# Cosine-similarity attention on one core: five score banks with exponentials of three and two tiles, joint row sums, and a scale scratch inside a value bank

## The chip, the cores and the metric

The kernel runs on one core of a Trainium2 chip. The metric is the device time of one execution in microseconds. A core has TensorE (PE, with its weight loads listed as PEld), VectorE (DVE), ScalarE (ACT), GpSimd (POOL) and SyncE (SP), which here only issues transfers. Each engine works through its own list of instructions in order, and the lists are tied together by semaphores. PSUM is used in eight banks of 512 float32 columns by 128 partitions.

## The reference

Q, K and V are (8, 12, 512, 64) in float32, tau is 0.1.

```python
Q_norm = Q / (np.linalg.norm(Q, axis=-1, keepdims=True) + 1e-10)
K_norm = K / (np.linalg.norm(K, axis=-1, keepdims=True) + 1e-10)
scores = np.einsum('bhqd,bhkd->bhqk', Q_norm, K_norm) / tau
weights = np.exp(scores - np.max(scores, axis=-1, keepdims=True))
weights = weights / (np.sum(weights, axis=-1, keepdims=True) + 1e-10)
return np.einsum('bhqk,bhkd->bhqd', weights, V).astype(np.float32)
```

The scores are at most 10 in size, so the kernel takes the exponential without subtracting the maximum.

## The kernel before

The 96 heads are worked in 48 pairs s of two heads h. The 512 rows of a head lie as four tiles of 128. For a pair the steps are these, with the names under which the program keeps them:

- LD, LV: Q, K and V of the pair come in by DMA on SP's queue (256 KB each). VC casts V to bf16 on POOL and sets it beside a column of ones.
- SQ: the squares of Q and K, mostly one POOL instruction over 1024 columns (line 395).
- SSQ and RED: the sums of squares over 64 columns. For K, PE adds eight strided slices with an identity matrix as weights into columns 320 to 383 of one of the two value banks (SSQ, line 416), and DVE reduces the remaining 8 to 1 (RED, line 423). For Q, DVE reduces the squares directly (line 427). Only the K sums of pairs 43 and 47 are taken directly too.
- NEW: the reciprocal square root of the sums of a group of pairs (sizes 1, 1, 1, 1, then 2, later 4), in eight or so small DVE instructions of a Newton iteration (lines 450 to 465). The iterate lives in a PSUM bank of its own, `n_bank`, where PE never writes. Groups 0 and 1 use a logarithm and an exponential on ACT instead (NRMS, LOG, lines 283 to 285 and 439 to 448).
- SCL: Q times its scale on DVE (line 482), K times its scale on POOL for 38 pairs and on DVE for nine (`K_ON_DVE`).
- TR and EVA: PE transposes both (line 488), DVE copies them out of PSUM (line 496, `qt`).
- SCO: scores of one key tile c for both heads, two matmuls with 64 rows each (line 590), into two of the four banks of `sc_ps`; the two sets of two banks take turns.
- EXP: ACT reads both banks and writes 1024 columns of `et` (line 606). The last tile of the last pair is cut in three pieces (line 601); the tiles of pair 0 are taken one head at a time, with K's scale as a column (line 582). One tile, (43, 3), is not done on ACT but as a polynomial on DVE and POOL.
- PV: values, four key tiles for each of four query tiles, 128x65 (line 626), into value bank h (`o_ps`); column 64 holds the sum of weights. RCP takes its reciprocal (line 638), NRM scales into `ob` (line 643), ST writes 256 KB back.

A score group waits for the exponential that used its banks last, and for EVA. A group of values waits for the exponentials of its pair and, for its first tile, for the NRM (and RED, where a sum was put there) that used the bank before:

```python
bank_free[s, h] = before[b]
before[b] = [("NRM", s, h)] + ([("RED",) + attached[s, h]] if (s, h) in attached else [])
```

The order on every engine is written out by hand as a list of numbers (`ORDER`); nothing is reordered at run time. PE opens with nine warming matmuls of 512 columns (line 209). In the head, ACT squares parts of pairs 0 and 1 and does the norms of pair 0 before the exponentials run.

Of the kernel before, what the change touches and what calls it, by code (L numbers as in the profile page):

```python
# [108 lines left out]
def bass_cosine_similarity_attention_kernel(  # L109
# [26 lines left out]
    et = [sb(f"et{i}", [128, NT, 2, SEQ], bf16) for i in range(R_ET)]  # L136
# [15 lines left out]
    sc_ps = nc.alloc_psum_tensor("scps", [128, 4, SEQ], f32)  # L152
# [5 lines left out]
    n_bank = nc.alloc_psum_tensor("nps", [128, 512], f32)  # L158
    n_ps = n_bank[:, 0 : R_X * MOST].rearrange("p (r x) -> p r x", r=R_X)
# [62 lines left out]
    slots = sorted((START + PERIOD * (s + 1) + 0.9 * PV_AT[4 * h + 3] + 0.05 + late(s), s, h) for s in range(NP - 1) for h in range(2))  # L222
    chunks = [(s, c) for s in range(NP) for c in range(NT) if (s, c) not in OFF]
    off_of = {s: c for s, c in OFF}
    poly_groups = {group[s] for s in off_of}
    turn_user, free_user = {}, []
    for (s, c), turns in OFF.items():
        for h in range(2):
            if turns[h] >= 0:
                turn_user.setdefault(turns[h], []).append((s, h))  # L230
            else:
                free_user.append((s, h))
    session, attached, early = {}, {}, []
    for s, w in sorted(((s, w) for s in range(NP) for w in range(2) if on_pe(s, w)), key=lambda j: (due_red(j[0]), j)):
        at = due_red(s) + 0.3
        if s < EARLY:
            early.append((s, w))
            continue
        due, i, h = next(x for x in slots if x[0] >= at and (x[1], x[2]) not in attached)
        attached[i, h] = (s, w)  # L240
        session[s, w] = (h, due, [("PV", i, h, NT - 1)])
    before = [[("EVA", 0, 1, 0), ("EVA", 0, 1, 1)], []]
    for s, w in sorted(early):
        b = w if s >= ONE_BANK else 0
# [4 lines left out]
    before["n"] = [("SCL", NP - 1, 0)] + [("X",) + u + (1,) for u in free_user]  # L249
    place = lambda s, h: VALUE_BANK.get((s, h), h if s < NP - 1 else (0, 1, "t")[h])  # L250
    for s in range(NP):
        for h in range(2 if s < NP - 1 else 3):
            b = place(s, h)
            bank_free[s, h] = before[b]
            before[b] = [("NRM", s, h)] + ([("RED",) + attached[s, h]] if (s, h) in attached else [])
    values = {0: o_ps[0], 1: o_ps[1], "t": x_ps, "n": n_bank[:, :]}

    def head0(TF):
        for h in range(2):
# [5 lines left out]
            if CAST0[h] == "act":  # L265
# [3 lines left out]
            P.add(("CST", 0, h), CAST0[h], "cst" + CAST0[h], at, [("LD", 0, 1, h)], emit)  # L269
            r_ps = sc_ps[:, 1, 0:4] if h == 0 else n_ps[:, 0, 0:4]  # L270
# [53 lines left out]
    def root(s, w):  # L324
# [3 lines left out]
        return 7 if w == 0 or s in K_ON_DVE else 6  # L328
# [11 lines left out]
    def together(s, dst, g):  # L340
        bank, due, before = session[s, 1]

        def ssq(e):
            for k in range(8):
                last = e.matmul(
                    out=o_ps[bank][:, 320:448], lhsT=ident[:, :], rhs=sq[s % R_SQ][:, :, 8 * k : 8 * k + 8],
# [6 lines left out]
                  out=dst, in_=o_ps[bank][:, 320:448].rearrange("p (w g e) -> p w g e", w=2, e=8), axis=AX.X, op=ALU.add))  # L353

    def pair(s):
# [73 lines left out]
        xg, tg, yg = xs[g % R_X][:, 0 : 2 * m], ts[g % R_X][:, 0 : 2 * m], n_ps[:, g % R_X, 0 : 2 * m]  # L429
# [19 lines left out]
        elif s == first[g]:  # L449
# [6 lines left out]
            def up(dst, lo, hi, c):  # L456
# [8 lines left out]
                7: up(yg, 0, 2 * m, c_g) if on_dve else up(rq_g, 0, m, c_g)}  # L465
            done = None
            for k in news(g):
                needs = [done] if k else reds + [("SCL", i, w) for i in past for w in range(2) if w == 0 or i in K_ON_DVE]
                if k == 0 and g == R_X:
# [41 lines left out]
    def exps(s, c):  # L511
        if s < 0:
            return []
        if s == NP - 1 and c == NT - 1:
            return [("EXP", s, c, k) for k in range(3)]
        if s == 0:
            return [("EXP", s, c, h) for h in range(2)]
        return [("Y", s, last_step(s, c)) if (s, c) in OFF else ("EXP", s, c)]

    def poly(s, c, at):  # L520
# [6 lines left out]
        for h in range(2):  # L527
            users = turn_user[turns[h]] if turns[h] >= 0 else free_user
            bank = x_ps if turns[h] >= 0 else n_bank[:, :]
            after = ("EVA", turns[h]) if turns[h] >= 0 else ("SCL", NP - 1, 0)  # L530
# [35 lines left out]
    def rest(s):  # L566
# [3 lines left out]
        for c in range(NT):  # L570
# [3 lines left out]
            if s == 0:  # L574
                for h in range(2):
                    rows = slice(64 * h, 64 * h + 64)
                    P.add(("SCO", 0, c, h), "pe", "sco1", 0.5 * (c + NT * h),
                          [("EVA", 0, w, h) for w in range(2)] + ([("EXP", 0, c, 0)] if h else []) + ([("SCL", 0, 0, 0)] if c == 1 else []),
                          lambda e, c=c, rows=rows: e.matmul(
                              out=sc_ps[:, c, :], lhsT=qt[iqt][rows, 1, c, :], rhs=qt[iqt][rows, 0, :, :], start=True, stop=True))  # L580
                    P.add(("EXP", 0, c, h), "act", "exps", 0.5 * (c + NT * h), [("SCO", 0, c, h), ("NRMS", 0, 1, h), "table"],
# [3 lines left out]
            turn = chunks.index((s, c))  # L585
            b = turn % 2

            def sco(e, c=c, b=b):
                for h in range(2):
                    last = e.matmul(  # L590
                        out=sc_ps[:, 2 * b + h, :], lhsT=qt[iqt][64 * h : 64 * h + 64, 1, c, :],
                        rhs=qt[iqt][64 * h : 64 * h + 64, 0, :, :], start=True, stop=True)
                return last

            used = [("EXP", 0, 2 * c + i, 1) for i in range(2)] if turn < NT + 2 else exps(*chunks[turn - 2])
            P.add(("SCO", s, c), "pe", "sco", T0 + 0.9 * c, [("EVA", s)] + used, sco)
            if last_pair and c == NT - 1:
                for k, (h, lo, hi) in enumerate(PIECES):
                    P.add(("EXP", s, c, k), "act", "exp1" if hi - lo == NT else "exph", T0 + 0.9 * c + 0.3 * k,
                          [("SCO", s, c)] + [key("PV", s - R_ET, i, NT - 1) for i in range(2)],  # L600
                          lambda e, c=c, b=b, h=h, q=slice(128 * lo, 128 * hi): e.activation(
                              out=et[iet][:, c, h, q], in_=sc_ps[:, 2 * b + h, q], func=ACT.Exp, scale=math.log(2.0) / UNIT if group[s] in poly_groups else inv_tau))
                continue
            P.add(("EXP", s, c), "act", "exp", T0 + 0.9 * c,
                  [("SCO", s, c)] + [key("PV", s - R_ET, h, NT - 1) for h in range(2)] + ["table"],
                  lambda e, c=c, b=b: e.activation(  # L606
# [261 lines left out]
```

## Time and profile before

| | |
|---|---|
| median of 3 runs | 190.34 us (189.74 to 190.72) |
| profiled execution | 189.61 us, its span 187.9 us |
| granted clock of PE | 0.998 |
| busy: PE / DVE / ACT / POOL | 175.1 / 169.3 / 181.8 / 160.9 us |
| exponentials of 1024 columns | 186 |
| value products / score products / sums on PE | 1504 / 374 / 384 in the trace |
| read and written | 37.75 MB and 12.58 MB |

In the rows of the profile a group stands as: line, engine, operation, output<-input, shapes, xcount, then busy time of the group in us, mean duration of one in ns, and idle time of the engine just before them with what ended it. In a row of the timeline: start and length in us from the start of the span, engine, line, tiles, and how many instructions were merged. Durations of neighbours overlap on ACT, PE and DVE, so a pitch is read from starts or from busy time over count. In a row of stretches: the stretch, its length, the busy time of PE, PEld, DVE, ACT and POOL with instruction counts, the granted clock, the busy share of DMA and GB/s.

### The profile page before, as it was taken

How to read it: one execution, taken by the hardware profiler on the slowest of the kernel's cores; microseconds unless marked ns; L12 is line 12 of the kernel's file. 1: busy time of each engine (PE TensorE's matmuls, PEld its weight loads, DVE VectorE, ACT ScalarE, POOL GpSimd, SP SyncE). 2: the span in 40 equal slices, each digit the busy share in tenths (PEclk: the TensorE clock that was granted, in tenths of full speed). 3: DMA queues.
4: the chain of work that ended last, by engine and by line, in shares of the span. 5: the costliest groups of instructions: out<-in, count | busy, mean ns of one | idle time of the engine just before them, and what ended most of it. 6: DMA issues, size and time to landing. Idle time of an engine off the chain costs nothing.

```text
span 187.9 us, 6658 instructions
## 1 busy us (share of the span) xinstructions
PE 175.1 (93%) x2705; PEld 110.8 (59%) x2705; DVE 169.3 (90%) x541; ACT 181.8 (97%) x215; POOL 160.9 (86%) x149
## 2 busy tenths in 40 slices
PE   8799799999999999999999989999999899899982
PEld 2455366566666666666666656556566566455652
DVE  1799999999999999999999998999989999998752
ACT  5799999999999999999999999999999999999993
POOL 4599999999999999999999999999999993594000
PEclk9999999999999999999999999999999999999999
DMA  5999999999997999999999999987973063200655
GB/s 143 345 351 351 348 348 371 367 382 336 310 293 265 282 303 320 289 365 287 366 381 367 369 372 364 364 292 213 341 240 117 13 210 101 74 0 3 212 183 169
DMA packets 52446, 50.76 MB, mean 270 GB/s; under 512 B 3136, under 2 KB 52416, under 8 KB 52416
## 3 DMA queue, kind: packets, MB, share of 16 engines
q1 hardware_dynamic: 51984, 50.02, 81.4%
q8 instruction: 21, 0.34, 0.8%
q10 hardware_dynamic: 432, 0.33, 0.5%
q14 instruction: 9, 0.07, 0.1%
HBM read 37.75 MB, written 12.58 MB: 268 GB/s over the span
## 4 chain that ended last, share of the span: by engine, by line
ACT 93%; DMA 3%; PE 2%; DVE 1%; SPq 0%; issue 0%
ACT et L606 89%; DMA qk<-in_Q_dram 3%; ACT et L582 3%; PE ops L626 1%; ACT sq L387 1%; PE ops L657 0%; SPq L366 0%; PE scps L590 0%; DVE ob L676 0%; DVE ob L643 0%; DVE rd L668 0%; ACT ya L439 0%; DVE rd L638 0%; PE tps L657 0%; ACT xa L285 0%
## 5 line engine op out<-in xcount | busy, mean ns | idle before, releaser
L606 ACT ACTIVATE et<-scps 128x1024 bf16<-128x1024 f32 x186 | 170.6, 1192 | 0.0
L395 POOL TENSOR_TENSOR sq<-qk 128x1024 bf16<-128x1024 f32 x44 | 82.8, 1899 | 0.2 <-DMA qk<-in_K_dram 0.2
L590 PE MATMUL scps<-qt 64*128 64x512 bf16 x374 | 73.0, 386 | 7.0 <-ACT et L606 3.6
L626 PE MATMUL ops<-vb,et 128*128 128x65 bf16 x1504 | 75.4, 195 | 0.1
L626 PEld LDWEIGHTS ops<-vb,et 128*128 128x128 bf16 x1504 | 57.2, 98 | 29.2 <-issue 17.9
L482 POOL TENSOR_TENSOR qn<-qk,rk 128x512 bf16<-128x512 f32 x38 | 39.4, 1048 | 5.4 <-DVE rk L457 5.1
L643 DVE TENSOR_TENSOR ob<-ops,rd 128x256 f32<-128x256 f32 x94 | 39.0, 419 | 0.7
L482 DVE TENSOR_TENSOR qn<-qk,nps 128x512 bf16<-128x512 f32 x56 | 36.9, 677 | 0.3
L496 DVE COPY qt<-tps 128x1024 bf16<-128x1024 bf16 x47 | 32.1, 683 | 0.9 <-PE tps L488 0.6
L488 PE MATMUL tps<-ident,qn 128*128 128x128 bf16 x376 | 32.3, 220 | 0.3 <-DVE qn L482 0.2
L590 PEld LDWEIGHTS scps<-qt 64*128 64x128 bf16 x374 | 18.5, 92 | 23.9 <-ACT et L606 8.1
L427 DVE TENSOR_REDUCE xs<-sq 128x8 f32<-128x512 bf16 x46 | 30.4, 671 | 0.2 <-POOL sq L395 0.2
L614 POOL TENSOR_SCALAR vb<-vf 128x512 bf16<-128x512 f32 x48 | 29.1, 627 | 0.0
L488 PEld LDWEIGHTS tps<-ident,qn 128*128 128x128 bf16 x376 | 21.5, 98 | 10.2 <-issue 5.2
L638 DVE RECIPROCAL rd<-ops 128x4 f32<-128x4 f32 x94 | 16.1, 175 | 5.0 <-PE ops L626 3.8
L416 PE MATMUL ops<-sq,ident 128*128 128x64 bf16 x384 | 19.0, 193 | 0.0
L416 PEld LDWEIGHTS ops<-sq,ident 128*128 128x128 bf16 x384 | 14.2, 98 | 4.0 <-issue 2.5
L423 DVE TENSOR_REDUCE xs<-ops 128x8 f32<-128x64 f32 x46 | 9.5, 208 | 0.5 <-PE ops L416 0.3
L457 DVE SCALAR_TENSOR_TENSOR nps<-ts,nps 128x32 f32<-128x32 f32 (+3 forms) x34 | 6.7, 196 | 0.5
L450 DVE TENSOR_TENSOR ts<-xs,nps 128x32 f32<-128x32 f32 (+2 forms) x34 | 6.6, 194 | 0.5
L453 DVE SCALAR_TENSOR_TENSOR ts<-ts,nps 128x32 f32<-128x32 f32 (+2 forms) x34 | 6.5, 190 | 0.4
L389 POOL TENSOR_TENSOR sq<-qk 128x512 bf16<-128x512 f32 (+1 forms) x5 | 4.7, 955 | 2.2 <-DMA qk<-in_K_dram 2.0
(60 smaller groups left out, 53.2 us busy)
## 6 DMA issues: line engine op xcount, KB each, us to landing
vf<-in_V_dram SPq DMA_DIRECT2D x48, 256.0 KB, 6.3
qk<-in_Q_dram SPq DMA_DIRECT2D x47, 256.0 KB, 5.1
qk<-in_K_dram SPq DMA_DIRECT2D x47, 256.0 KB, 6.2
out_dram<-ob SPq DMA_DIRECT2D x47, 256.0 KB, 5.0
qk<-in_Q_dram SPq DMA_DIRECT2D x2, 128.0 KB, 2.7
qk<-in_K_dram ACTq DMA_DIRECT2D x2, 128.0 KB, 2.9
out_dram<-ob SPq DMA_DIRECT2D x1, 128.0 KB, 1.7
out_dram<-ob ACTq DMA_DIRECT2D x1, 64.0 KB, 1.8
```

The costliest lines, as they stand in the source:

```text
L395: lambda e: e.tensor_tensor(out=sqf, in0=data, in1=data, op=ALU.mult))
L416: last = e.matmul(out=o_ps[bank][:, 320:384], lhsT=ident[:, :], rhs=sq[iqs][:, 8 * w : 8 * w + 8, 8 * k : 8 * k + 8], start=(k == 0), stop ...
L427: lambda e, w=w, dst=dst: e.tensor_reduce(out=dst, in_=sq[iqs][:, 8 * w : 8 * w + 8, :], axis=AX.X, op=ALU.add))
L482: lambda e, w=w, r=r: e.tensor_tensor(out=qn[iqn][:, w].rearrange("p t h d -> p h t d"), in0=qk[iq][:, w].rearrange("p h (t d) -> p h t d" ...
L488: last = e.transpose(t_ps[:, w, t, :], qn[iqn][:, w, t].rearrange("p h d -> p (h d)"), ident[:, :])
L496: lambda e: e.tensor_copy(out=qt[iqt][:, :, :, :].rearrange("p w t x -> p (w t x)"), in_=t_ps[:, :, :, :].rearrange("p w t x -> p (w t x)")))
L590: last = e.matmul(out=sc_ps[:, 2 * b + h, :], lhsT=qt[iqt][64 * h : 64 * h + 64, 1, c, :], rhs=qt[iqt][64 * h : 64 * h + 64, 0, :, :], sta ...
L606: lambda e, c=c, b=b: e.activation(out=et[iet][:, c, :, :], in_=sc_ps[:, 2 * b : 2 * b + 2, :], func=ACT.Exp, scale=math.log(2.0) / UNIT i ...
L614: lambda e: e.tensor_scalar(out=vb[:, ivb : ivb + n, :, :, 0:DIM].rearrange("p n h c d -> p (n h c) d"), in0=vf[:, iv : iv + n].rearrange( ...
L626: last = e.matmul(out=values[place(s, h)][:, 65 * t : 65 * t + 65], lhsT=et[iet][:, c, h, 128 * t : 128 * t + 128], rhs=vb[:, ivb, h, c, : ...
L638: lambda e, h=h, grid=grid: e.reciprocal(out=rd[io][:, h, :], in_=grid[:, :, DIM]))
L643: lambda e, h=h, grid=grid: e.tensor_tensor(out=ob[io][:, h], in0=grid[:, :, 0:DIM], in1=rd[io][:, h, :].unsqueeze(2).to_broadcast([128, N ...
```

## The change

Five things are edited together, with a new written order for every engine.

1. `sc_ps` has five banks instead of four. From pair 8 on, single score tiles (s, c, h) are grouped by threes in banks 0 to 2 and twos in banks 3 and 4, in turn; a group may go over a pair's end, but not over the wrap of the ring of `et`, which is now one tensor. Pairs 1 to 7 keep twos. Each group is one SCO and one EXP. Two cuts remain: tile (43, 3), which is a polynomial, and the last tile.
2. `n_bank` is gone. The Newton iterate of the first six groups lies in score bank 4 (`n_head`), that of later ones in the last 128 columns of value bank 1. There, a step or scaling which touches the bank is put between the NRM of one pair's head 1 and the first value product of the next pair's head 1: the step waits for that NRM, and that value product waits for the step (`in_window`). Steps 0 to 3 of a group lie in one such window, steps 4 to 7 in the next, the scaling of Q four pairs ahead.
3. For 21 pairs (`SUMMED_TOGETHER`) PE sums Q and K in one set of eight products of 128 columns, and DVE reduces both at once. The sums from pair 4 on all go into value bank 0. The K sums of pairs 20 and 21, instead of 43 and 47, are taken directly on DVE.
4. K of 17 pairs instead of nine is scaled on DVE. Where another pair of the group is scaled by POOL, DVE reads the scale that POOL uses.
5. Three dummy products of 512 columns (`FILLS`): one behind the warming products, two behind the first exponential.

Also the ring of loaded Q and K has 16 places instead of 17, that of cast V 14 instead of 16. `SECOND_SCALED` is empty, so its branches do nothing.

```diff
-    et = [sb(f"et{i}", [128, NT, 2, SEQ], bf16) for i in range(R_ET)]
+    et_all = sb("et", [128, R_ET * NT * 2, SEQ], bf16)
+    et = [et_all[:, 2 * NT * i : 2 * NT * (i + 1), :].rearrange("p (c h) q -> p c h q", h=2) for i in range(R_ET)]
...
-    sc_ps = nc.alloc_psum_tensor("scps", [128, 4, SEQ], f32)
+    sc_ps = nc.alloc_psum_tensor("scps", [128, 5, SEQ], f32)
...
-    n_bank = nc.alloc_psum_tensor("nps", [128, 512], f32)
-    n_ps = n_bank[:, 0 : R_X * MOST].rearrange("p (r x) -> p r x", r=R_X)
+    n_ps = both[:, :, 512 - 2 * MOST : 512].rearrange("p b (r x) -> p b r x", x=MOST)
+    n_head = sc_ps[:, 4, :].rearrange("p (r x) -> p r x", x=MOST)
...
+    def fill(n):
+        return lambda e: e.matmul(out=sc_ps[:, 0, 0:n], lhsT=one(128), rhs=one(n), start=True, stop=True)
+
+    for k, (late_one, n) in enumerate(FILLS):
+        P.add(("FILL", k), "pe", f"fill{n}", 8.5 if late_one else 4.5, [("EXP", 0, 0, 0)] if late_one else [], fill(n))
...
         def ssq(e):
             for k in range(8):
                 last = e.matmul(
-                    out=o_ps[bank][:, 320:448], lhsT=ident[:, :], rhs=sq[s % R_SQ][:, :, 8 * k : 8 * k + 8],
+                    out=o_ps[bank][:, 260:388], lhsT=ident[:, :], rhs=sq[s % R_SQ][:, :, 8 * k : 8 * k + 8],
...
+    def in_window(key, w, b):
+
+        if w < 0:
+            window_ops.setdefault((0, b), []).append(key)
+            return [("RED", s, 1) for s in range(1, ONE_BANK)]
+        window_ops.setdefault((w + 1, b), []).append(key)
+        return [("NRM", w, b)]
...
+                if g > HEAD_GROUPS:
+                    needs = needs + in_window(done, max(first[g] - LEAD_STEP[k], summed_at.get(g, -1)), norm_bank(g))
...
+    def unit(u):
+        halves, bank = units[u]
...
+        def sco(e):
+            for i, (s, c, h) in enumerate(halves):
+                last = e.matmul(
+                    out=sc_ps[:, bank + i, :], lhsT=qt[s % R_QT][64 * h : 64 * h + 64, 1, c, :],
+                    rhs=qt[s % R_QT][64 * h : 64 * h + 64, 0, :, :], start=True, stop=True)
+            return last
...
+        P.add(("EXP", u), "act", {1: "exp1h", 2: "exp", 3: "exp3"}[n], T0, [("SCO", u), "table"] + free,
+              lambda e: e.activation(out=et_all[:, at : at + n, :], in_=sc_ps[:, bank : bank + n, :], func=ACT.Exp, scale=scale))
...
+    for (s, b), keys in window_ops.items():
+        P.ops["PV", s, b, 0].needs += keys
...
+FILLS = ((0, 512), (1, 512), (1, 512))
...
-BY_VECTOR = (43, 47)
+BY_VECTOR = (20, 21)
-K_ON_DVE = (1, 2, 4, 9, 15, 21, 27, 33, 39)
+K_ON_DVE = (1, 2, 3, 4, 6, 9, 12, 15, 18, 21, 24, 27, 30, 33, 36, 39, 42)
-RINGS = (17, 8, 16, 6, 4, 4, 5, 8, 3)
+RINGS = (16, 8, 14, 6, 4, 4, 5, 8, 3)
-ONE_BANK = 0
+ONE_BANK = 3
+LEAD_SCALE = 4
+LEAD_STEP = (6, 6, 6, 6, 5, 5, 5, 5)
+LEAD_SUM = 6
+FIRST_WIDE = 8
+HEAD_GROUPS = 5
-SUMMED_TOGETHER = ()
+SUMMED_TOGETHER = (4, 5, 6, 7, 8, 9, 10, 11, 12, 14, 16, 18, 22, 24, 26, 28, 30, 32, 34, 36, 38)
```

More of the change, by code (lines that the diff above doesn't have):

```diff
@@ L254, in bass_cosine_similarity_attention_kernel @@
             bank_free[s, h] = before[b]
-            before[b] = [("NRM", s, h)] + ([("RED",) + attached[s, h]] if (s, h) in attached else [])
-    values = {0: o_ps[0], 1: o_ps[1], "t": x_ps, "n": n_bank[:, :]}
+            before[b] = [("NRM", s, h)] + [("RED",) + x for x in attached.get((s, h), [])[-1:]]
+    values = {0: o_ps[0], 1: o_ps[1], "t": x_ps}
     def head0(TF):
@@ L468, in pair @@
                 needs = [done] if k else reds + [("SCL", i, w) for i in past for w in range(2) if w == 0 or i in K_ON_DVE]
+                if k == 0 and g > HEAD_GROUPS and slot_users[norm_bank(g)].index(g) >= 2:
+                    old = slot_users[norm_bank(g)][slot_users[norm_bank(g)].index(g) - 2]
+                    needs += [("SCL", i, w) for i in range(first[old], first[old] + sizes[old]) for w in range(2) if w == 0 or i in K_ON_DVE]
                 if k == 0 and g == R_X:
@@ L499, in pair, with first_tile @@
         rest(s)
+    def first_tile(c, h):
+        return c // 2 * 2 if h and SECOND_SCALED else c
     def scos(s):
@@ L527, in poly @@
         for h in range(2):
[L528 to L530 removed]
+            users, bank, after = turn_user[turns[h]], x_ps, ("EVA", turns[h])
             before = [("X",) + users[users.index((s, h)) - 1] + (1,)] if users.index((s, h)) else []
@@ L584, in rest @@
                 continue
[L585 to L606, printed above, removed]
-                      out=et[iet][:, c, :, :], in_=sc_ps[:, 2 * b : 2 * b + 2, :],
-                      func=ACT.Exp, scale=math.log(2.0) / UNIT if group[s] in poly_groups else inv_tau))
+            for h in range(2):
+                if units[unit_of[s, c, h]][0][0] == (s, c, h):
+                    unit(unit_of[s, c, h])
         n = len(cast_with[s])
@@ L730, in on_pe, with exp_groups, norm_bank, sum_bank @@
     return 0 < s < PE_BOTH or s >= EARLY and (s not in BY_VECTOR if w else s in Q_ON_PE)
+def exp_groups(NP, NT):
+    runs, run = [], []
+    for s in range(1, NP):
+        for c in range(NT):
+            for h in range(2):
+                if (s, c) in OFF or (s, c) == (NP - 1, NT - 1):
+                    if run:
+                        runs.append(run)
+                    run = []
+                    continue
+                if run and (s % RINGS[6] == 0 and run[-1][0] != s or s == FIRST_WIDE and run[-1][0] != s):
+                    runs.append(run)
+                    run = []
+                run.append((s, c, h))
+    if run:
+        runs.append(run)
+    runs.append([(NP - 1, NT - 1, 0), (NP - 1, NT - 1, 1)])
+    units, odd = [], 0
+    for run in runs:
+        best = {(0, odd): (0, None)}
+        for n in range(len(run)):
+            for o in range(2):
+                if (n, o) not in best:
+                    continue
+                most = 2 if o or run[0][0] < FIRST_WIDE or run is runs[-1] else 3
+                for k in range(1, most + 1):
+                    if n + k <= len(run):
+                        cost = best[n, o][0] + (1 if k > 1 else 1.5)
+                        if (n + k, 1 - o) not in best or cost < best[n + k, 1 - o][0]:
+                            best[n + k, 1 - o] = (cost, (n, o, k))
+        ends = (0,) if run[-1][0] == FIRST_WIDE - 1 else (0, 1)
+        at = min(((len(run), o) for o in ends if (len(run), o) in best), key=lambda x: best[x][0])
+        path = []
+        end = at[1]
+        while best[at][1] is not None:
+            n, o, k = best[at][1]
+            path.append((run[n : n + k], (2 if run[0][0] < FIRST_WIDE else 3) * o))
+            at = (n, o)
+        units += path[::-1]
+        odd = end
+    return units, {x: u for u, (halves, bank) in enumerate(units) for x in halves}
+def norm_bank(g):
+    return 0 if g in FIRST_BANK else 1
+def sum_bank(g):
+    return 0
 def late(s):
```

118 lines of the change are left out of this document (83 added, 35 removed), and 159 rows, old and new, of the table ORDER.

## The prediction

> **What bounds the kernel now.** First the page's head, then the chain of work that ended last, its answer in order of time, and stretches of the span.
>
> ```profile
> span 187.9 us, 6658 instructions
> PE 175.1 (93%) x2705; PEld 110.8 (59%) x2705; DVE 169.3 (90%) x541; ACT 181.8 (97%) x215; POOL 160.9 (86%) x149
> ACT 93%; DMA 3%; PE 2%; DVE 1%; SPq 0%; issue 0%
> 12.97 167.76 ACT et L606 x183
> 14.00:28.00 14.00, 12.47 (x188) 7.64 (x188) 13.51 (x49) 14.00 (x16) 13.66 (x12) 1.00 1.10 349
> 42.00:78.00 36.00, 35.20 (x589) 23.35 (x587) 35.15 (x126) 36.00 (x41) 35.87 (x31) 1.00 0.97 302
> 78.00:174.00 96.00, 92.04 (x1441) 58.58 (x1438) 91.53 (x270) 96.00 (x107) 88.06 (x78) 1.00 0.73 242
> ```
>
> The chain is one engine: from 12.97 us on, 183 exponentials follow each other for 167.76 us, 0.917 us each. The stretches (columns: length, then PE, PEld, DVE, ACT, POOL, granted clock, DMA) show ACT without a hole. PE, DVE and POOL are each at 95% or more between 42 and 78 us, so work cannot be moved freely. Head (13 us) and tail (from 183.2 us on) lie outside.
>
> **What an exponential costs beside its columns.**
>
> ```profile
> L606 ACT ACTIVATE et<-scps 128x1024 bf16<-128x1024 f32 x186 | 170.6, 1192 | 0.0
> L601 ACT ACTIVATE et<-scps 128x512 bf16<-128x512 f32 x1 | 0.8, 768 | 0.0
> 183.19 1.32 ACT L601 ACTIVATE et<-scps 128x512 bf16<-128x512 f32 x3
> L582 ACT ACTIVATE et<-scps,xa 128x512 bf16<-128x512 f32 x8 | 4.9, 678 | 0.0
> L606 ACT ACTIVATE et<-scps x186: 1017/1222/1319, 12.8 to 182.3; 128x1024 bf16<-128x1024 f32 x186
> ```
>
> The mean duration of 1192 ns overlaps the next instruction; what counts is busy over count, 170.6 / 186 = 0.917 us for 1024 columns. The last pair's three pieces take 1.32 us, the first of 512 columns 0.768 by itself; the other two, 256 columns each, add (1.32 - 0.768) / 2 = 0.276. So a column costs (0.917 - 0.276) / 768 = 0.835 ns and an instruction 0.276 - 256 x 0.835 = 0.062 us on top. The eight of pair 0 give 4.9 / 8 = 0.61 for 512 and so a fixed part of 2 x 0.61 - 0.917 = 0.31, but they read their scale from a tile (xa), which the others don't. I take 0.062, from the instructions of the same form, and keep 0.31 as the other end.
>
> The Trainium skill (ScalarE: Activation LUTs, "What ACT_TABLE_LOAD costs") gives 186 ns + 0.833 ns a column with immediate scale, and neighbours that overlap by 93 ns, thus 93 ns fixed. By that 1024 columns would take 0.946 us; the 0.917 here is shorter and decides. By the page the next paragraph's gain would be 2.8 us.
>
> **ACT, the gain.** Counted in the grouping: pairs 1 to 7 keep 28 exponentials of two tiles. From pair 8 a run of five pairs (the ring of `et` has five) has 40 tiles in eight threes and eight twos instead of twenty twos; with the breaks at pairs 10, 43, 44 and the last there are 60 threes and 96 twos, 156 in place of 186. 30 fewer x 0.062 = **-1.9 us**. A three takes 1.343 (0.062 + 1536 x 0.835 ns), a three and a two 2.26, a pair 1.6 x 2.26 = 3.616 instead of 4 x 0.917 = 3.667.
>
> **PE, more work.**
>
> ```profile
> 58.96 0.39 PE L590 MATMUL scps<-qt 64*128 64x512 bf16 x2
> 59.28 0.43 PE L626 MATMUL ops<-vb,et 128*128 128x65 bf16 x8
> 59.55 0.39 PE L416 MATMUL ops<-sq,ident 128*128 128x64 bf16 x8
> 59.88 0.39 PE L590 MATMUL scps<-qt 64*128 64x512 bf16 x2
> 60.20 0.40 PE L488 MATMUL tps<-ident,qn 128*128 128x128 bf16 x4
> 60.43 0.42 PE L626 MATMUL ops<-vb,et 128*128 128x65 bf16 x8
> 60.79 0.39 PE L590 MATMUL scps<-qt 64*128 64x512 bf16 x2
> 6.54 1.03 PE L579 MATMUL scps<-qt 64*128 64x512 bf16 x4
> ```
>
> Here PE runs through without waiting, so starts give prices. Two score products (rows 0-63 and 64-127) run at once: the whole takes 0.39, as one does, and 0.32 passes until the next work starts. Eight value products take 0.27 (0.033 each), four transposes 0.23, eight sums of 64 columns 0.33 to the next scores. Entering the scores costs 0.36 - 8 x 0.033 = 0.09 extra, so a group of two costs 0.41. In a three the third shares its rows with the first and cannot run beside it: +(1.03 - 0.39) / 3 = 0.21, thus 0.62. Scores: 187 groups x 0.41 = 77.2 before; 97 x 0.41 + 60 x 0.62 = 77.7 after; the third product gives back what the fewer entries save. A joint sum streams 128 columns where K alone streamed 64: a transpose of that width takes 0.056, a sum now 0.029, so 8 x 0.027 = 0.21 more, x 21 = +4.4 us. PE in all: +4.8 us of issue, against ACT -1.9.
>
> Per pair with a joint sum in the region of threes: 8 x 0.132 values + 2 x 0.23 transposes + 8 x 0.056 sums + (3.2 x 0.41 + 1.6 x 0.21) scores = 3.6 us, against ACT's 3.616. With a K sum alone 3.4; before, 3.4 against 3.667. Joint sums belong to pairs 4 to 12, then to about every second one to 38, and run some six pairs ahead, at pairs 2 to 30: there PE is 97 to 100% full.
>
> **The refill of a three.**
>
> ```profile
> 38.08 0.39 PE L590 MATMUL scps<-qt 64*128 64x512 bf16 x2
> 38.51 1.03 ACT L606 ACTIVATE et<-scps 128x1024 bf16<-128x1024 f32 x1
> 39.60 0.39 PE L590 MATMUL scps<-qt 64*128 64x512 bf16 x2
> ```
>
> The scores end at 38.47 and ACT starts on them at 38.51: 0.04. It ends at 39.54, and the next scores into its banks start at 39.60: 0.06. The shortest exponential takes 1.017. A bank of two comes round in 0.06 + 0.39 + 0.04 + 1.02 = 1.51, while ACT's own round is 2 x 0.917 = 1.83: PE may come 0.32 late without ACT losing. For a three: 0.06 + 0.60 + 0.04 + (1.02 + 0.43) = 2.15 against 2.26: 0.11. So the change takes two thirds of the cushion away at each of 60 threes, while PE has less idle time to be punctual with. The twos in between gain one (0.75). Lower end: 0, since the fuller stretch now (35.20 of 36 us busy) cost ACT nothing. Upper end: before, PE has 0.28 us per pair to wait in (3.667 - 3.388); with joint sums 0.0 to 0.2. If it needs all 0.28, some 27 pairs lose 0.15 on average, 4 us. I take **+0.6**, near the lower end, because that is the row of the same stretch.
>
> **DVE and POOL.**
>
> ```profile
> L427 DVE TENSOR_REDUCE xs<-sq 128x8 f32<-128x512 bf16 x46 | 30.4, 671 | 0.2 <-POOL sq L395 0.2
> L423 DVE TENSOR_REDUCE xs<-ops 128x8 f32<-128x64 f32 x46 | 9.5, 208 | 0.5 <-PE ops L416 0.3
> L482 DVE TENSOR_TENSOR qn<-qk,nps 128x512 bf16<-128x512 f32 x56 | 36.9, 677 | 0.3
> L482 POOL TENSOR_TENSOR qn<-qk,rk 128x512 bf16<-128x512 f32 x38 | 39.4, 1048 | 5.4 <-DVE rk L457 5.1
> L453 DVE SCALAR_TENSOR_TENSOR ts<-ts,nps 128x32 f32<-128x32 f32 (+2 forms) x34 | 6.5, 190 | 0.4
> L643 DVE TENSOR_TENSOR ob<-ops,rd 128x256 f32<-128x256 f32 x94 | 39.0, 419 | 0.7
> L638 DVE RECIPROCAL rd<-ops 128x4 f32<-128x4 f32 x94 | 16.1, 175 | 5.0 <-PE ops L626 3.8 <-PE ops L416 0.5
> ```
>
> 21 Q reductions go: -21 x 0.671. The joint reduction reads 128 columns instead of 64: +64 x (671 - 208) / 448 ns = 0.07, x 21 = +1.4. Eight more K scalings: +8 x 0.677 = +5.4 on DVE, -8 x 1.048 = -8.4 on POOL. DVE -7.3, POOL -8.4; neither is on the chain, so 0 of it counts. It is room for what is new: the Newton steps' scratch and the scale factors move into the last columns of value bank 1, so the first value product of (s+1, head 1) now waits, beside the NRM of (s, 1), for one Q scaling in every pair and for four steps in the windows of groups 6 to 18 (two each, 26). Queued behind it on PE are the next scores. Nothing before shows this wait. One round of that bank: scaling 0.68 + four steps 4 x 0.19 + four value groups 0.53 and 0.19 of pipeline + reciprocal 0.18 + NRM 0.42 = 2.8 of 3.616. Other DVE work in between (copy of qt 0.68, the other head's reciprocal and NRM 0.6, a reduction 0.27 to 0.67) is 1.6 to 2.0, of which the value products cover 0.7: the round closes between 3.7 and 4.1 if all of it lies inside, and at 2.8 if none does. The durations overlap by some 0.08 per instruction (on DVE 0.1 to 0.2 us each would be too low), over twelve instructions 1 us, so it fits by a little. Cost: 0; the upper end is among the rivals.
>
> **Head, DMA, rings.**
>
> ```profile
> 0.82 4.00 PE L209 MATMUL ops<-const-bfloat16-1.0 128*128 128x512 bf16 x9 [0.82 <-PEq L850]
> 3.69 0.40 ACT L266 ACTIVATE qn<-qk 128x256 bf16<-128x256 f32 x1
> 4.75 0.64 PE L299 MATMUL ops<-ident,qn 128*64 128x128 bf16 x4
> 6.56 0.63 ACT L387 ACTIVATE sq<-qk 128x512 bf16<-128x512 f32 x1 [1.13 <-DMA qk<-in_Q_dram]
> 9.37 0.60 PE L579 MATMUL scps<-qt 64*128 64x512 bf16 x2 [0.91 <-DVE qt L310]
> ```
>
> The first dummy stands right behind the warming products, which already keep the transposes waiting (cast done at 4.09, start 4.75), so it delays them by one such product, (4.00 - 0.63) / 8 = 0.42. The cover is ACT's wait of 1.13 for Q of pair 1, which ends at 6.56; without it 0.42 is paid. The DVE order now copies before it takes K's second sum, and ACT takes that sum's logarithm ahead of the square: this uses up the cover and gives back 0.3 later. 0 taken, -0.3 to +0.4. The other two dummies wait for the first exponential and lie where PE stood idle for 0.91 before 9.37: 0. Loads keep their order with a ring of 16 pairs instead of 17, the cast V of 14 instead of 16; DMA moves less after 78 us (share 0.73), so 0.
>
> **The sum**, against the profiled execution's own 189.61 (span 187.9 and 1.7 around it): -1.9 + 0.6 + 0 = 188.3. That execution lies 0.73 below the median of 190.34; on the median 189.0.
>
> **Rivals.**
> 1. The refill eats the gain: lateness of PE costs 1.3 to 2.8 instead of 0.6; 189.7 to 191.2 on the median, no change at 190.3. For it: PE at 97 to 100%, cushion 0.11. Against: full stretches lose nothing now, and twos have 0.75 to catch up in.
> 2. Slower: the windows in bank 1. PE waits at the head-1 values for the steps; each lost 0.07 in 26 windows is the whole gain. At 0.15 each: +3.9, so -1.9 + 0.6 + 3.9 on 190.34 = 192.9; at 0.1, 191.6. For it: the round closes only thanks to overlaps. Against: DVE is 7 us emptier.
> 3. A larger fixed part: with 30 x 0.31 = 9.3 ACT would be done before PE, whose busy 175.1 + 4.8 = 180 stands in the way; with 30 x 0.12 and no lateness, 186.7. For it only the row of another form. The skill's 93 ns named above would lie here too.
>
> **How the numbers follow.** Less than 0.5% (about 0.95 us) can't be told from no change here. Forecast (187.9 to 189.4): 0.45; rival 1: 0.3, mostly inside 0.5%; rival 2: 0.18; rival 3: 0.07. Faster 0.50, same 0.28, slower 0.22. For 8 in 10 the range goes from 187.8 (no lateness and a little more) to 191.5 (windows at 0.1); the forecast's own range is 187.9 to 189.4.
>
> **What would show it.** Right: 60 threes at about 1.34 us of pitch, no idle ACT, L606's successor near 168.7 us busy in total; PE busy about 98% with more score waits on ACT gone; DVE near 162, POOL near 152. Wrong by rival 1: idle before threes ended by score products, longest between 20 and 110 us. By rival 2: value products waiting for `qn` scaling or `nps` steps, and ACT holes behind them. By 3: threes under 1.30.

## The result and the profile after

The changed kernel takes **198.68 us** (197.7 to 198.99, 6 runs) against 190.14 of the kernel before beside it: a ratio of 1.0449, 95% interval 1.0426 to 1.0471. 189.0 was forecast, in a range from 187.8 to 191.5, with 0.22 for slower. The prediction is wrong, in its sign too. The profiled execution takes 198.99, its span 197.0. Times below are medians of all executions of a kernel, and ratios leave out the few executions in which the whole kernel ran in a slower state.

The head of the page after, with the chain by engine:

```profile
span 197.0 us, 6623 instructions
PE 180.3 (92%) x2708; PEld 110.9 (56%) x2708; DVE 178.1 (90%) x527; ACT 182.7 (93%) x185; POOL 158.9 (81%) x141
DVE 32%; PE 32%; ACT 23%; issue 4%; DMA 3%; POOL 3%; SPq 2%
```

The stretch from 42 to 78 us after (columns as before: length, then PE, PEld, DVE, ACT, POOL, granted clock, DMA share, GB/s):

```profile
42.00:78.00 36.00, 32.83 (x525) 20.79 (x524) 35.30 (x111) 33.12 (x31) 35.51 (x30) 1.00 0.94 306
```

Before, ACT alone held 93% of the chain and was busy 36.00 of these 36 us. Now it is busy 33.12, and a third of the chain is DVE. PE is where it was forecast (180.3 for 179.9); DVE, forecast near 162, is at 178.1.

The groups of the page after, for exponentials, scalings of Q and K, and squares:

```profile
L595 ACT ACTIVATE et<-scps 128x1024 bf16<-128x1024 f32 (+1 forms) x156 | 171.2, 1211 | 7.9 <-PE scps L566 7.4
L514 DVE TENSOR_TENSOR qn<-qk,ops 128x512 bf16<-128x512 f32 x40 | 27.3, 683 | 0.7
L514 DVE TENSOR_TENSOR qn<-qk,rk 128x512 bf16<-128x512 f32 x14 | 20.5, 1466 | 0.0
L514 POOL TENSOR_TENSOR qn<-qk,rk 128x512 bf16<-128x512 f32 x30 | 33.3, 1119 | 12.9 <-DVE rk L483 12.9
L421 POOL TENSOR_TENSOR sq<-qk 128x1024 bf16<-128x1024 f32 x44 | 84.5, 1932 | 0.2 <-DMA qk<-in_K_dram 0.2
```

Fourteen scalings on DVE last 1466 ns on average, where forty of the same shape last 683. The difference is in the tile that gives the scale: `ops` lies in PSUM, `rk` in SBUF. These fourteen are the K of pairs that share a group with a pair scaled on POOL. The waits of the kernel after (in all, times, longest):

```profile
PEld tps L520 <- DVE qn L514: 9.7, 14, 1.8
ACT et L595 <- PE scps L566: 7.4, 13, 1.4
PE tps L520 <- DVE qn L514: 5.8, 8, 1.5
PE ops L361 <- POOL sq L421: 0.8, 1, 0.8
```

PE's weight loads for the transposes wait fourteen times for DVE's scalings, and ACT thirteen times for scores. The last line is one wait for POOL itself: at 22.20 us PE stands 0.79 for a square, and the exponential behind it, at 23.19, comes 0.74 late. In the timeline, the K of pair 15 and, as the last line, that of pair 39:

```profile
59.05 7.89 POOL L421 TENSOR_TENSOR sq<-qk 128x1024 bf16<-128x1024 f32 x4
59.08 2.41 DVE L514 TENSOR_TENSOR qn<-qk,rk 128x512 bf16<-128x512 f32 x1
62.07 0.69 DVE L514 TENSOR_TENSOR qn<-qk,ops 128x512 bf16<-128x512 f32 x1
62.82 0.62 PE L520 MATMUL tps<-ident,qn 128*128 128x128 bf16 x8 [1.52 <-DVE qn L514]
64.01 2.37 ACT L595 ACTIVATE et<-scps 128x1536 bf16<-128x1536 f32 x2 [1.44 <-PE scps L566]
...
150.90 0.66 DVE L514 TENSOR_TENSOR qn<-qk,rk 128x512 bf16<-128x512 f32 x1
```

POOL begins its squares at 59.05, DVE its scaling 0.03 later; the scaling ends at 61.49, 0.55 after the first square (59.05 + 1.89). What stands behind it on DVE is late, then the transposes, then ACT, by 1.44. The scaling at 150.90 has no POOL instruction beside it and takes 0.66.

**Where the 9.1 us of span went.** Before, the ends of successive exponentials are 0.9165 apart for two tiles, without a late one; after, undisturbed pitches are 0.9165 and 1.3435. Taking these off every distance between ends, and summing what is left wherever it is over 0.06, gives the time by which exponentials came late: 0 before, 10.3 after. The rest of the stretch from the first exponential of 1024 columns to the end of the last one is 170.6 before and 168.75 after, -1.9; that first one starts 0.44 later (12.85 before, 13.29 after), and the tail is 0.2 longer. Together +9.1. "Late" below is this sum.

### The profile page after: what moved, and what is told of

Same layout as the page of the kernel before. It is cut to its first block, busy times and chain, and to the rows that moved or that the text cites. A ratio compares the mean times of both kernels' runs of the same rounds, so it can differ in the third digit from the quotient of the medians.

```text
span 197.0 us, 6623 instructions
## 1 busy us (share of the span) xinstructions
PE 180.3 (92%) x2708; PEld 110.9 (56%) x2708; DVE 178.1 (90%) x527; ACT 182.7 (93%) x185; POOL 158.9 (81%) x141
## 4 chain that ended last, share of the span: by engine, by line
DVE 32%; PE 32%; ACT 23%; issue 4%; DMA 3%; POOL 3%; SPq 2%
ACT et L595 23%; PE ops L686 12%; PE scps L566 12%; DVE qn L514 11%; DVE ob L703 7%; PE tps L520 4%; DVE qt L528 4%; DVE xs L453 3%; DMA qk<-in_Q_dram 3%; PE ops L361 3%; DVE rd L698 2%; POOL sq L421 2%; DVE ts L476 1%; PE ops L442 1%; SPq L395 1%
## 5 line engine op out<-in xcount | busy, mean ns | idle before, releaser
L595 ACT ACTIVATE et<-scps 128x1024 bf16<-128x1024 f32 (+1 forms) x156 | 171.2, 1211 | 7.9 <-PE scps L566 7.4
L421 POOL TENSOR_TENSOR sq<-qk 128x1024 bf16<-128x1024 f32 x44 | 84.5, 1932 | 0.2 <-DMA qk<-in_K_dram 0.2
L686 PE MATMUL ops<-vb,et 128*128 128x65 bf16 x1504 | 71.2, 195 | 1.6 <-DVE ob L703 0.9
L514 POOL TENSOR_TENSOR qn<-qk,rk 128x512 bf16<-128x512 f32 x30 | 33.3, 1119 | 12.9 <-DVE rk L483 12.9
L514 DVE TENSOR_TENSOR qn<-qk,ops 128x512 bf16<-128x512 f32 x40 | 27.3, 683 | 0.7
L514 DVE TENSOR_TENSOR qn<-qk,rk 128x512 bf16<-128x512 f32 x14 | 20.5, 1466 | 0.0
L453 DVE TENSOR_REDUCE xs<-sq 128x8 f32<-128x512 bf16 x25 | 16.8, 671 | 0.0
L361 PE MATMUL ops<-sq,ident 128*128 128x128 bf16 x168 | 12.9, 219 | 0.9 <-POOL sq L421 0.8
L361 PEld LDWEIGHTS ops<-sq,ident 128*128 128x128 bf16 x168 | 9.6, 98 | 3.4 <-issue 2.0
L442 PE MATMUL ops<-sq,ident 128*128 128x64 bf16 x216 | 10.6, 193 | 0.6 <-POOL sq L415 0.5
L442 PEld LDWEIGHTS ops<-sq,ident 128*128 128x128 bf16 x216 | 8.0, 98 | 4.0 <-POOL sq L415 1.9
L514 DVE TENSOR_TENSOR qn<-qk,scps 128x512 bf16<-128x512 f32 x10 | 6.5, 678 | 0.6 <-ACT scps L469 0.6
```

What stands on the lines that cost most here:

```text
L361: last = e.matmul(out=o_ps[bank][:, 260:388], lhsT=ident[:, :], rhs=sq[s % R_SQ][:, :, 8 * k : 8 * k + 8], start=(k == 0), stop=(k == 7))
L421: lambda e: e.tensor_tensor(out=sqf, in0=data, in1=data, op=ALU.mult))
L442: last = e.matmul(out=o_ps[bank][:, 320:384], lhsT=ident[:, :], rhs=sq[iqs][:, 8 * w : 8 * w + 8, 8 * k : 8 * k + 8], start=(k == 0), stop ...
L453: lambda e, w=w, dst=dst: e.tensor_reduce(out=dst, in_=sq[iqs][:, 8 * w : 8 * w + 8, :], axis=AX.X, op=ALU.add))
L514: lambda e, w=w, r=r: e.tensor_tensor(out=qn[iqn][:, w].rearrange("p t h d -> p h t d"), in0=qk[iq][:, w].rearrange("p h (t d) -> p h t d" ...
L595: lambda e: e.activation(out=et_all[:, at : at + n, :], in_=sc_ps[:, bank : bank + n, :], func=ACT.Exp, scale=scale))
```

## Experiments

The theories: **A**, DVE's scaling of K from `rk` waits until POOL's running instruction has read, and the lateness goes on to PE and ACT. **B**, the steps and scalings in value bank 1. **C**, the refill of the exponentials of three.

**e1: the same 14 from PSUM.** The last Newton step of a mixed group writes to `ops` too, and the fourteen read that; each then holds value bank 1 until it ends.

```diff
-            from_bank = dve and not (w and not acts and on_pool(g))
+            from_bank = dve
...
+                P.ops["PV", before_it[1] + 1, 1, 0].needs.append(("SCL", s, 1))
```

> The changed kernel, with one operand put back: the 14 K scalings on DVE in groups where POOL scales another pair read their scale from the PSUM scratch, as in the kernel before, and not from the SBUF tile rk; step 7 writes the K half too (widths only), and each such scaling is ordered in bank 1 against the value products next to it in the written order. Theory A (a DVE instruction with both inputs in SBUF waits for the POOL instruction that runs, 1.47 us instead of 0.68): the 14 scalings fall to 0.68, DVE loses 11 us of busy time, ACT's idle falls from 7.9 to under 2 us, time 188 to 190.5. Theory B (the windows of bank 1 hold PE): the scalings fall but the value products still wait for steps and Q scalings; time over 195. Theory C (the refill of the threes): holes before threes remain, 194 to 197.

201.45 us, ratio 1.061 (1.058 to 1.064), late 11.8: not A's 188 to 190.5, but B's over 195. The group of the scalings that read `ops` (line numbers are one higher here):

```profile
L515 DVE TENSOR_TENSOR qn<-qk,ops 128x512 bf16<-128x512 f32 x52 | 35.4, 681 | 0.7
```

And the waits of e1:

```profile
PEld ops L687 <- DVE qn L515: 14.0, 14, 1.7
ACT et L596 <- PE scps L567: 9.8, 13, 1.3
```

The slow scalings are gone (681 ns), the time isn't. The first value group of head 1 now waits for the K scaling, which stands late in DVE's order. e1 puts a wait of B's kind where A's was, so the time does not tell the two apart; the 681 shows only that the slow scalings hang on the operand.

**e2: the kernel before, with the wait put in.** Seven of its nine K scalings on DVE read `rk` instead of `nps`; no threes, no windows. The Newton step that writes `rk` now also stands behind earlier K scalings on DVE, which DVE's own order gives anyway.

```diff
-        return 7 if w == 0 or s in K_ON_DVE else 6
+        return 7 if w == 0 or not on_pool(g) else 6
...
-            r = (rkd[:, c8 : c8 + 8] if dve else rk_g[:, c8 : c8 + 8]) if w else rq_g[:, c8 : c8 + 8]
+            r = (rkd[:, c8 : c8 + 8] if dve and (acts or not on_pool(g)) else rk_g[:, c8 : c8 + 8]) if w else rq_g[:, c8 : c8 + 8]
```

> The kernel before, with that operand alone changed: the seven K scalings on DVE in mixed groups (pairs 4, 9, 15, 21, 27, 33, 39) read the scale from the SBUF tile rk instead of PSUM. No other edit. Theory A: these seven take 0.66 us where POOL is idle and up to 2.4 where a square runs, 1.5 in the mean; DVE busy +5.5 us; ACT, without a hole before, gets holes at some of the seven; time 190.1 plus 2 to 6. Theories B and C: no effect, 190.1 within 0.5%.

209.89, ratio 1.102 (1.092 to 1.112), late 19.6, far more than the 2 to 6 expected. The group of the seven:

```profile
L482 DVE TENSOR_TENSOR qn<-qk,rk 128x512 bf16<-128x512 f32 x7 | 22.3, 3190 | 0.0
```

The longest of them in the timeline of e2, with POOL's rows:

```profile
105.68 1.03 POOL L482 TENSOR_TENSOR qn<-qk,rk 128x512 bf16<-128x512 f32 x1
105.84 7.45 DVE L482 TENSOR_TENSOR qn<-qk,rk 128x512 bf16<-128x512 f32 x1
106.69 1.19 POOL L614 TENSOR_SCALAR vb<-vf 128x512 bf16<-128x512 f32 x2
107.86 3.73 POOL L395 TENSOR_TENSOR sq<-qk 128x1024 bf16<-128x1024 f32 x2
111.56 1.19 POOL L614 TENSOR_SCALAR vb<-vf 128x512 bf16<-128x512 f32 x2
```

The operand alone, without anything else of the change, costs 19.6 us of span (207.5 against 187.9). This scaling lets seven POOL instructions past and ends 0.54 after the last (111.56 + 1.19). Theory A holds; B and C do not exist in this kernel.

Not all of the 19.6 is the wait itself. The clock row of the page of e2 (forty slices of 5.2 us, tenths of full clock):

```profile
PEclk9999999999998799999996699999999679999998
```

PE's granted clock is 0.50 from 66.4 to 69.8, from 110.8 to 117.6 and from 161.9 to 168.8 us, beside or behind the three longest scalings; in the kernel after it is 1.00 all along. In these three stretches the exponentials behind the first late one come late as well, by 2.9 us together. How much the lower clock adds was not separated.

**e3: the 14 scalings on POOL**, `K_ON_DVE = (1, 2, 3)`, each ahead of the next later K scaling in POOL's order.

> The changed kernel, with the 14 K scalings of mixed groups taken from DVE's list and put into POOL's, each ahead of the next later K scaling there. Theory A: no DVE instruction has two SBUF inputs any more, DVE busy falls by 20 us, POOL takes 14.7 more (174 busy, close to full, some scalings late); time 189 to 193. Theory B: windows remain, over 195. Theory C: 194 to 197.

205.98, ratio 1.087 (1.082 to 1.092), late 16.2, far outside A's 189 to 193. DVE's busy time falls to 162.5, but in the waits of e3 PE's transposes stand behind POOL:

```profile
PEld tps L520 <- POOL qn L514: 14.1, 10, 3.3
ACT et L595 <- PE scps L566: 14.0, 14, 3.3
```

The four longest late starts (3.5, 1.9, 1.7 and 2.8 us) come behind the transposes of K of pairs 9, 15, 21 and 27, whose scaling stands late in POOL's order. Here too the granted clock is lower: 0.50 for 3.4 us behind three of the four, 0.975 in the mean.

**e4 and e5: short squares.** POOL's squares read 64 of 1024 columns from pair 10 on (the others are left out), in the kernel after (e4) and, as a control, in the kernel before (e5).

```diff
-                  lambda e: e.tensor_tensor(out=sqf, in0=data, in1=data, op=ALU.mult))
+                  lambda e, n=1024 if s < 10 else 64: e.tensor_tensor(out=sqf[:, 0:n], in0=data[:, 0:n], in1=data[:, 0:n], op=ALU.mult))
```

> The changed kernel, with the POOL squares from pair 10 on cut to 64 of their 1024 columns (the rest of the squares is left out; every instruction, wait and order stays). POOL then holds nothing long while a K scaling with two SBUF inputs runs on DVE. Theory A (the 14 scalings wait for POOL's running instruction): they fall from 1.47 to 0.7 to 1.0 us, ACT's late starts fall from 10.3 to under 3 us in total, time 189 to 192. Theories B and C (bank-1 windows, refill of the threes): time stays over 195, since nothing of theirs is touched.

> Control for the run before: the kernel before with the same squares cut (the rest of the squares left out). If POOL's work as such holds nothing up, the time stays at 190.1 within 0.5%, and what the cut saves in the changed kernel is the waiting on DVE. If it falls by more than 1 us, that much of the other run's gain is POOL's own.

e4: 192.94, ratio 1.016 (1.013 to 1.019), late 3.7; the fourteen fall to 1016 ns. All three figures lie just above what A expected (under 3, 0.7 to 1.0 us, 189 to 192); B and C had the time over 195. e5: 189.86, ratio 1.001 (0.998 to 1.004). POOL's squares hold up nothing in the kernel before, and cost 5.7 us in the kernel after. The group of the fourteen in e4:

```profile
L514 DVE TENSOR_TENSOR qn<-qk,rk 128x512 bf16<-128x512 f32 x14 | 14.2, 1016 | 0.0
```

**e6: e1 with 12 of the K scalings earlier in DVE's order**, right behind the last Newton step they need or the scaling of Q in the same window.

> The kernel of e1 (K scale read from PSUM), with 12 of the K scalings moved on DVE to the earliest place in their bank-1 window: right behind the last step they need, or behind the window's Q scaling. In e1 eleven value groups start 0.06 us after such a scaling ends. If that gate is what e1 lost (11.8 us of late ACT starts), each is paid 0.5 to 1.3 us sooner: time 193 to 197, under e1's 201.5. If e1's loss is the refill of the threes, no change.

194.86, ratio 1.025 (1.023 to 1.028), late 5.5: inside the 193 to 197 expected. PE's weight loads for values still wait 8.0 us for DVE's scalings (14.0 in e1).

**e7: dummy products of one column**, `FILLS = ((0, 1), (1, 1), (1, 1))`.

> The changed kernel, with the three dummy products cut from 512 columns to 1. The prediction had their cost at 0, -0.3 to +0.4. After the change the first 1024-column exponential starts at 13.29 us of the span, 12.85 before. If the first dummy delays the transposes: it starts at 12.8 to 12.9 and the time falls by 0.4 (198.3). If it is the new order in the head: 13.3 stays.

198.69, ratio 1.045 (1.041 to 1.050): the dummies do not make the 8.5 us.

**e8 and e10: POOL again.** e8 is e3 with K of pairs 9, 15, 21 and 27 right behind that of 8, 14, 20 and 25 in POOL's order. In e10 one more pair of entries is swapped in PE's order of the head, written here by name (pair, key tile, head; pair, Q or K):

```diff
-("SCO", 0, 2, 1), ("SSQ", 2, 1), ("SCO", 0, 1, 1), ("TR", 1, 1)
+("SCO", 0, 2, 1), ("SCO", 0, 1, 1), ("SSQ", 2, 1), ("TR", 1, 1)
```

> As the kernel after with the 14 scalings of K on POOL, but those of pairs 9, 15, 21 and 27 stand earlier in POOL's order, right behind the scaling of the pair ahead of them. In the run with all 14 on POOL the exponentials started 16.2 us late in sum, 12.6 of it at these four pairs. Theory A (the loss is the wait of DVE's scaling for POOL's reads of SBUF; on POOL the scaling costs only POOL's time, if it comes in time): the four late starts go and the time is 190 to 196. Theory B (the loss is the refill of the exponentials of three and the steps in value bank 1, whoever scales K): 197 or more. Theory C (POOL is too full with 14 more scalings, 167 of the span, wherever they stand): the late starts move to other pairs, 200 or more.

> As the run with the early scalings on POOL, and in PE's order of the head the second score product of pair 0's second key tile stands ahead of the sums of squares of pair 2, which wait for POOL's squares of a Q that lands at 10.2 us. Theory A (the first exponential of 1024 columns starts at 13.3 instead of 12.85 because that product stands behind these sums): it starts at 12.7 to 13.0 and the time is 0.3 to 0.8 below that of the run with the early scalings. Theory B (the head ends with DVE's copies or the data, whatever PE's order): start within 0.1 of that run, time the same.

202.87 (1.054 to 1.071) and 202.84 (1.049 to 1.074). The stretch from 78 to 127 us in e8:

```profile
78.00:127.00 49.00, 43.64 (x679) 27.57 (x679) 39.98 (x123) 45.49 (x40) 49.00 (x44) 1.00 0.98 324
```

Its timeline at the costliest case:

```profile
122.60 3.74 POOL L421 TENSOR_TENSOR sq<-qk 128x1024 bf16<-128x1024 f32 x2
126.30 2.04 POOL L514 TENSOR_TENSOR qn<-qk,rk 128x512 bf16<-128x512 f32 x2
127.39 0.61 PE L520 MATMUL tps<-ident,qn 128*128 128x128 bf16 x4 [3.58 <-POOL qn L514]
```

POOL has no hole in 49 us, and K comes late at another pair, 3.4 us at 128.6: the third theory of e8. These two are better than e3 and worse than the change itself, so on POOL the fourteen cost more than their wait on DVE, a lower clock behind the long waits included (0.980 and 0.983). The head in e10 is not earlier than in e8 (13.70 against 13.35), but the two differ ahead of it: the warming products took 4.00 us in e10 and 3.92 in e8, and the first transposes begin at 5.18 and 4.89. In other runs where they begin at 5.17 or 5.18, the first exponential starts at 13.68 to 13.86.

**e9: as e4, squares short from pair 6 on.**

```diff
-n=1024 if s < 10 else 64
+n=1024 if s < 6 else 64
```

> As the kernel after, but POOL's squares take only 64 of 1024 columns from pair 6 on instead of pair 10 on; the other squares are left out, so the sums are not those of the data. With the cut from pair 10 on 192.9 was measured and 3.7 us of late starts, 2.1 of it behind the scalings of K of pairs 4 and 6, which still met full squares. Theory A (each scaling waits for the POOL instruction that is running): both shrink, 190.5 to 192, late starts 1.5 to 2.5 in sum, which is then what the refill and the steps in bank 1 cost (0.6 was forecast). Theory B (these late starts belong to the first exponentials of three and the full stretch of PE): no change, 192.5 to 193.5.

193.04, ratio 1.013 (1.007 to 1.019), late 3.9: no gain over e4, so A missed its number here, and B's 192.5 to 193.5 held. But the scalings that stay long are not those beside squares, as the timeline of e9 shows at the K of pair 4:

```profile
21.31 1.04 POOL L514 TENSOR_TENSOR qn<-qk,rk 128x512 bf16<-128x512 f32 x1 [0.37 <-DVE rk L483]
21.35 1.55 DVE L514 TENSOR_TENSOR qn<-qk,rk 128x512 bf16<-128x512 f32 x1
```

One Newton step releases POOL's scaling and DVE's at once; DVE comes 0.04 later and waits for the whole of it.

**e11: POOL's own scalings short as well** (32 of 512 columns; the rest left out).

```diff
-                  lambda e, w=w, r=r: e.tensor_tensor(
+                  lambda e, w=w, r=r, n=DIM if dve else 4: e.tensor_tensor(
```

> As the kernel after with POOL's squares cut to 64 of 1024 columns from pair 6 on, and with POOL's own scalings of K cut to 32 of 512 columns as well; the other squares and scaled columns are left out. With the squares alone cut, 193.0 was measured and 3.9 us of late starts; in that run the longest of the 14 scalings on DVE (1.55, 1.55, 1.51, 1.38 us) began within 0.2 us of a POOL scaling that reads the same scale. Theory A (DVE's scaling waits for whichever POOL instruction is reading): the 14 fall to about 0.7 us, the late starts to 1.0 to 1.8 in sum, and the time to 189.8 to 191.3, which is then the change without the wait: within 1% of the kernel before. Theory B (what is left of the late starts is the refill of the exponentials of three and the steps in bank 1): no change, 192.6 to 193.4.

**190.36**, ratio 1.0021 (1.0006 to 1.0035), late 1.36. The page of e11, its head and two groups:

```profile
PE 179.6 (95%) x2708; PEld 111.2 (59%) x2708; DVE 168.8 (89%) x527; ACT 181.1 (96%) x185; POOL 66.3 (35%) x141
L595 ACT ACTIVATE et<-scps 128x1024 bf16<-128x1024 f32 (+1 forms) x156 | 169.6, 1225 | 0.6 <-PE scps L566 0.3
L514 DVE TENSOR_TENSOR qn<-qk,rk 128x512 bf16<-128x512 f32 x14 | 10.6, 755 | 0.0
```

The fourteen are at 755 ns, ACT's wait for scores falls from 7.4 us to 0.3, and 8.3 us of time are gone. In the kernel after PE's matmuls never wait for POOL's own scalings; once the exponentials of 1024 columns run, they wait for POOL twice, 0.8 and 0.1 us, both times for squares. In the kernel before (e5) nothing is held up by the squares. So what the short reads took away is DVE's wait, but for about a microsecond of late exponentials behind that one square (0.74, 0.09 and 0.38 from 23.19 us on). With e2, where the operand alone slows a kernel that has nothing else of the change, this settles A: neither the threes nor the joint sums nor bank 1 made the change slow, but fourteen instructions that read two operands from SBUF while POOL reads.

**e12: e11 with dummies of one column**, the edit of e7.

> As the run with POOL's squares and scalings cut short (the rest left out; 190.36 us, ratio 1.0021, first exponential of 1024 columns at 13.85, 0.97 to 1.07 behind the kernel before), with the three dummy products at 1 column instead of 512. Theory A (the first dummy delays the transposes of pair 0, and nothing covers it, 0.43 us; PE's order in the head costs the other 0.6): first exponential at 13.4, time 189.8 to 190.1, ratio 0.998 to 1.001. Theory B (the dummy is covered, as forecast): 13.7 to 13.9 and 190.2 to 190.6.

190.16, ratio 0.9997 (0.9967 to 1.0026). The first exponential of 1024 columns starts at 13.35 instead of 13.85, as A expected; the time lies between both ranges, and the interval of the ratio is too wide to settle it. PE's timeline in the head of e11, the first dummy and the first transposes:

```profile
4.61 0.63 PE L217 MATMUL scps<-const-bfloat16-1.0 128*128 128x512 bf16 x1
5.17 0.64 PE L315 MATMUL ops<-ident,qn 128*64 128x128 bf16 x4
```

The same transposes in e7, without the dummy:

```profile
4.75 0.63 PE L315 MATMUL ops<-ident,qn 128*64 128x128 bf16 x4
```

The dummy moves the transposes from 4.75 to 5.17, and the first exponential from 13.42 (e7) to 13.85 (e11), by 0.43. In e4 and e9, with the same dummy and transposes at 5.17 or 5.18, that exponential starts at 13.74 and 13.68, so up to 0.2 of the 0.43 may be scatter. In e12 the nine warming products took 3.90 us, 0.1 less than in e7 and e11, so 0.07 of its gain in the head is not the dummy's.

No version run here is faster than the kernel before.

## Why the prediction was wrong, point by point

**The step that failed is the term "+8 x 0.677 = +5.4 on DVE".** It took the K scalings at the price of the row `qn<-qk,nps`, whose scale lies in PSUM. Point 4 of the change says that in mixed groups DVE reads the scale that POOL uses, and the profile before names that tile `rk`, a tile in SBUF. No row before showed DVE at two SBUF operands beside a busy POOL: the nearest, `et<-xw,xz`, 1226 ns, had waited for POOL and ran alone. So the price was unknown and had to be bounded: at the lower end 0.677, at the upper end that price plus the rest of a POOL instruction, up to 1.899, on fourteen instructions and not on eight. Half a square at each, an estimate for a POOL that always runs squares, would have given 14 x 0.95 = 13 us on DVE, by this row of the page before:

```profile
L395 POOL TENSOR_TENSOR sq<-qk 128x1024 bf16<-128x1024 f32 x44 | 82.8, 1899 | 0.2 <-DMA qk<-in_K_dram 0.2
```

Measured: 20.5 - 14 x 0.683 = **+10.9 us** on DVE, and up to 9.0 us of late exponentials (10.3 in sum, 1.36 with the wait gone; about 1 of the difference stands behind POOL's square).

**"Neither is on the chain, so 0 of it counts" failed with it.** DVE had room on average, 178.1 of 197.0. But most of the fourteen are a long hole in DVE's order with transposes of a pair behind it, and ACT is fed through that order. None of the three rivals had this mechanism; the 0.22 for slower came from another one.

**The Trainium skill** (SBUF — State Buffer, "SBUF: two separate sides") says that a DVE instruction with two SBUF inputs and a GpSimd instruction that reads SBUF take turns at one shared pair of ports, and whichever starts first holds it for its whole length. The trace agrees: 2.41 beside squares, 0.66 with POOL idle. From that page alone one would end the wait with the POOL instruction under way; in e2 one scaling let seven of them past, so the rows decide that it can be longer.

**DVE, -7.3: too large even without the wait.** e11 has 168.8 busy, not 162; 14 x (0.755 - 0.683) = 1.0 of it is left of the wait. Most of the rest is overlap: the durations of all DVE instructions add up to 202.6 us before and 197.2 in e11, 5.4 less, but they overlap by 33.3 us before and 28.4 in e11, so the busy time falls by only 0.5. The forecast subtracted durations from busy time. POOL, 152 forecast, is at 158.9: its squares grew from 1899 to 1932 ns, its scalings from 1048 to 1119 and its casts from 627 to 657.

**ACT's gain, -1.9: right.** The pitches give (1.3435 - 0.9165) / 512 = 0.834 ns a column and 0.9165 - 1024 x 0.834 ns = 0.062 us fixed, as forecast; 30 x 0.062 is the -1.9 of the accounting above. The third rival is out. The Trainium skill (ScalarE: Activation LUTs, "What ACT_TABLE_LOAD costs") gives 186 ns beside the columns and an overlap of 93 ns between neighbours; the estimate from it is 0.093 fixed. The trace does not agree, and the pitch of the threes decides.

**PE, +4.8: right** (+5.2 after, +4.5 in e11). The sums on PE went from 19.0 us busy to 12.9 + 10.6, which is +4.5 for the +4.4 forecast. The printed prices give 76.7 and 77.0 for the scores, not 77.2 and 77.7, which changes little.

**Refill and windows, +0.6: inside the bounds, rivals 1 and 2 small.** With the wait gone, all lateness is 1.36: over twice the 0.6 taken, far from the 4 of the upper end. 0.40 of it is one place, the switch to the first three at 43.6 us (at pair 9: 32 twos come before it, so pair 8 is still in twos); the other seven are 0.06 to 0.21. Which of them are refill and which bank 1 was not separated.

**Head, 0 (-0.3 to +0.4): wrong.** The first exponential of 1024 columns starts at 12.78 to 12.85 in kernels with the head of before, at 13.29 to 13.86 in nine with the changed head and full dummies. The 0.42 of the first dummy is paid, at least in part (0.43 between e7 and e11, 0.26 between e7 and e9), and about 0.57 more remains without it (13.42 against 12.85). In e7, e11 and after itself ACT waits 0.7 to 0.8 for the last score product of pair 0. Putting that product ahead of the sums of pair 2 (e10) cut this wait to 0.39, but the exponential still starts at 13.70; so these sums are at most a part of it, and the rest of the cause is open. In the profiled execution after, the nine warming products took 3.51 us, not 4.00, which hid some of it (13.29).

**So the forecast's own sum would have failed by less**: without the wait, -1.8 + 1.4 + 1.0 of head + 0.3 of tail = +0.9, which is what the spans of e11 and before say (188.8 and 187.9). The change without the wait, and without most of POOL's reading, is 0.1 to 0.4% slower than before, no change by the bound of the prediction. That is where the first rival had put it, but partly by luck: 1.0 of what ate the gain comes from the head, which that rival did not have.

## What to carry to other kernels

Price an elementwise instruction by where its operands lie, not by its shape. Here a DVE instruction with both inputs in SBUF, run beside a POOL that is busy 81% of the span, cost its own 0.66 us and about what was left of POOL's instruction, or more (1.47 on average, 7.45 at worst in e2), and what stood in order behind it was late. On a kernel whose DVE, PE and ACT each run at 90% and more, count such instructions one by one before averages are compared.

## What the runs showed of the hardware that was not expected

A waiting DVE scaling usually got in after the POOL instruction under way (2.41 beside a square), and POOL's next one was then longer (2.34 instead of 1.89). But in e2 three of seven took 3.4, 6.4 and 7.45 us, past two to seven POOL instructions in a row. What decides between the two wasn't found. When DVE comes first, POOL waits: in e9 and e11 casts of 0.62 us that began 0.01 to 0.04 after a scaling took 1.13 to 1.15, and the scaling kept its 0.68.

PE's granted clock fell to 0.50 for 3.4 to 6.9 us beside long waits in e2, e3, e8 and e10. Which waits do this was not found: in e3 the transposes waited 1.55 us at 93.5 and the clock fell, 2.71 us at 120.4 and it did not.
